# Attention in a four-layer decoder trunk: transposes of probabilities and their products with values, two PSUM banks per step

## The chip, the cores and the metric

The kernel runs on one core of a Trainium2 chip. The metric is the device time of one execution in microseconds. The core has a matrix engine (TensorE; PE in the profile, with PEld for its weight loads), VectorE (DVE), ScalarE (ACT), GpSimd (POOL), and SyncE (SP), whose queue issues most DMAs. Each engine works through its own list of instructions in order. Matrix products and transposes run on PE and write to PSUM, which has 8 banks of 128 partitions by 512 fp32 values.

## The reference

Four layers over an input of 512 tokens by 1024 channels. Each layer is an RMS norm, a token mixer and a residual sum, then a norm, a conv-gated feed-forward block and a residual sum. The mixers are dilated attention (8 heads, three groups), latent attention (16 heads), differential attention (8 heads with two softmax maps each), and sliding-window attention (16 query heads, 2 key heads). Every mixer ends in a product of softmax probabilities with values. The differential one, cut to its core:

```python
def diff_attention(h, w_in, q_norm, k_norm, ..., subln, w_out, table, layer_idx):
    proj = h @ w_in
    q = rms_norm(proj[..., :qk_w].reshape(b, s, DIFF_HEADS, 2, HEAD_DIM), q_norm)
    k = rms_norm(proj[..., qk_w:2 * qk_w].reshape(b, s, DIFF_HEADS, 2, HEAD_DIM), k_norm)
    ...
    def block(args):
        ...
        logits = jnp.einsum('bqhmd,bkhmd->bhmqk', q_blk, k) * (HEAD_DIM ** -0.5)
        logits = jnp.where(dist >= 0, logits + bias, -jnp.inf)
        p = jax.nn.softmax(logits, axis=-1)
        a = p[:, :, 0] - lam * p[:, :, 1]
        return jnp.einsum('bhqk,bkhe->bqhe', a, vf)
    ...
    o = rms_norm(o, subln) * (1.0 - lam_init)
    return o.reshape(b, s, DIFF_HEADS * 2 * HEAD_DIM).astype(h.dtype) @ w_out
```

## The kernel before

The layers run as eight stages one after another: m0, f0, m1, f1, m2, f2, m3, f3 (m is a mixer, f a feed-forward block). Big products split each fp32 operand into a high and a low part and add three products, so names come in pairs (`wh`/`wl` for weights, `xh`/`xl` for the input, `oh`/`ol` for a mixer's output, `qh`/`ql` for queries or keys).

Each stage is written as cooperating generators ("tasks"). `round` advances all live tasks by one step, and a step ends at a `yield`. Buffers come from rings: `take` waits until one of the ring is free, `give` frees one. PSUM has four rings: `a` (3 banks, big products), `lg` (2, logits), `tr` (2, transposes), `av` (1, products with values). A row `a<-wh,xh` of the profile is thus a product into a bank of ring `a`. The tasks give the order in which the program is written. After that, a list scheduler of the language with its own estimate of times sets the final order of instructions on each engine, so moving a step can move rows on every engine, the DMA issues on SP among them.

One head of a mixer runs through these steps, here with the lines of m2:

- The input products land in a bank of ring `a`; `head_norm` (L843 to L853: a reduce on DVE, a chain of small rows, and the product with the scale) writes the normalized `nt`.
- `turn` (L863) transposes `nt` into a `tr` bank, once for the query (`mirror`) and once for the key (`ident`), and splits it into `qh` and `ql`. `stack` (L883) copies these by DMA on SP into `sk` tiles. Other DMAs on SP are the bias tiles (`bs`, L441) and the weight tiles (`wraw`, L254).
- `logits`: the products `lg<-sk` (L302, the line of every product); DVE adds the bias and finds the maximum (`p<-lg,bs`, L909); ACT takes the exponential (L284).
- m2 alone: DVE takes the reciprocals of the sums (L1045) and joins the two maps (L1049, L1050).
- `weigh`: it goes over groups of up to four 128x128 blocks of probabilities. It transposes a group into a `tr` bank (L961, `tr<-mirror,p`), ACT copies the bank to an SBUF tile `ptf` (L956; ring of 3), and PE multiplies it with the values into the `av` bank. Each of the three happens one step later than the one before it, for successive groups, so three groups are in hand at a time. Heads of m0, m1, m2 and m3 have 4, 5, 3 and 4 groups; each mixer calls `weigh` 8 times. `turn` numbers keep the heads in order.
- m2 alone: `head_norm` again, over the `av` bank, writes `ot` (L853), and `turn` transposes it (L863, `tr<-ident,ot`) into `oh` and `ol`.

The products with values have 64 columns of the stationary operand in m0, m1 and m3 and 128 in m2. Products of fp32 operands (`av<-ptf,v` and `av<-v,ptf`, `lg<-sk`) appear in the trace as two records where the program has one.

Of the kernel before, what the change touches and what calls it, by code (L numbers as in the profile page):

```python
# [13 lines left out]
AF = mybir.ActivationFunctionType  # L14
# [81 lines left out]
class Builder:  # L96
# [844 lines left out]
    def weigh(self, groups, turn):  # L941


        nc = self.nc
        ng = len(groups)
        tb, th = {}, {}
        while self.weighing != turn:
            yield
        for i in range(ng + 2):
            if i >= 2:  # L950
                yield from groups[i - 2][1](th[i - 2])
                self.give("ptf")
            if 1 <= i <= ng:
                n = 128 * len(groups[i - 1][0])
                th[i - 1] = yield from self.take("ptf")
                nc.scalar.activation(th[i - 1][:, :n], tb[i - 1][:, :n], AF.Copy)  # L956
                self.give("tr")
            if i < ng:
                tb[i] = yield from self.take("tr")
                for j, blk in enumerate(groups[i][0]):  # L960
                    nc.tensor.transpose(tb[i][:, j * 128:(j + 1) * 128], blk, self.mirror)  # L961
            if i == ng + 1:
                self.weighing += 1
            yield
# [962 lines left out]
```

## Time and profile before

| | |
|---|---|
| median of 3 runs | 2389.44 us (2388.29 to 2394.17) |
| profiled execution | 2390.37 us, span 2388.6 us |
| PE busy | 2331.5 us (98%), 16116 records |
| DVE busy | 1769.0 us (74%) |
| ACT busy | 1280.5 us (54%) |
| POOL busy | 315.4 us (13%) |
| mean granted TensorE clock | 0.99 |

All stretches and starts are microseconds from the start of the span. The stages lie at: m0 0 to 341, f0 to 722, m1 to 926, f1 to 1270, m2 to 1546, f2 to 1890, m3 to 2058, f3 to the end; neighbours overlap a little. A granted clock of 1.00 is the full clock of TensorE.

### The profile page before, as it was taken

What the parts mean: (1) busy time and instruction counts of PE and PEld (TensorE: products, weight loads), DVE (VectorE), ACT (ScalarE), POOL (GpSimd) and SP (SyncE); (2) the same over time, 40 slices, a digit from 0 to 9 for tenths busy, and PEclk for the clock granted to TensorE, in tenths of its full rate; (3) what the DMA queues carried; (4) which work ended last, traced back from release to release, by engine and by line L of the source; (5) the groups of instructions that cost most, each with busy time, mean ns of one, the idle gap of its engine ahead of it and who ended that gap; (6) DMA issues with size and microseconds to landing.
All of it is one profiled execution on the core that took longest, in us unless ns stands there. A gap on an engine that the chain in (4) does not pass through costs nothing.

```text
span 2388.6 us, 41006 instructions
## 1 busy us (share of the span) xinstructions
PE 2331.5 (98%) x16116; PEld 2115.6 (89%) x16116; DVE 1769.0 (74%) x3152; ACT 1280.5 (54%) x2378; POOL 315.4 (13%) x242
## 2 busy tenths in 40 slices
PE   8999989999999999999999998899999999999999
PEld 8999969999997768999989997799999987899998
DVE  6565688787768759877786666798777686987775
ACT  5555555444557756544454554464445575644443
POOL 0000022122002102222100000222220000222220
PEclk9999999999999999999999999999999999999999
DMA  5232255554221126555425454455552442655532
GB/s 181 82 98 89 89 141 164 154 150 133 78 93 45 34 65 173 159 154 151 120 94 159 133 137 113 141 162 150 148 149 76 139 108 91 173 159 158 155 115 84
DMA packets 98160, 298.43 MB, mean 125 GB/s; under 512 B 12144, under 2 KB 18480, under 8 KB 97968
## 3 DMA queue, kind: packets, MB, share of 16 engines
q1 hardware_dynamic: 85296, 249.67, 32.9%
q0 software_dynamic: 12672, 46.14, 11.0%
q8 instruction: 127, 2.08, 0.4%
q14 instruction: 65, 0.53, 0.1%
HBM read 273.62 MB, written 4.32 MB: 116 GB/s over the span
## 4 chain that ended last, share of the span: by engine, by line
PE 93%; DVE 3%; ACT 2%; DMA 1%; issue 1%; SPq 0%; POOL 0%; DVEq 0%; ACTq 0%; POOLq 0%
PE a L302 49%; PE tr L302 19%; PE lg L302 17%; PE av L302 3%; PE tr L961 2%; PE tr L863 2%; DVE r L628 1%; ACT wh L239 0%; DMA sk<-ql 0%; DVE wl L242 0%; DMA sk<-qh 0%; ACT xh L456 0%; DVE acc L466 0%; DMA x<-in_x_dram 0%; DVE xl L463 0%
## 5 line engine op out<-in xcount | busy, mean ns | idle before, releaser
L239 ACT ACTIVATE wh<-wraw 128x1024 fp32r<-128x1024 f32 (+3 forms) x357 | 358.0, 1008 | 493.6 <-PE a L302 216.5
L242 DVE TENSOR_TENSOR wl<-wraw,wh 128x1024 fp32r<-128x1024 f32 (+3 forms) x357 | 441.6, 1239 | 150.9 <-ACT wh L239 149.9
L302 PE MATMUL a<-wh,xh 128*128 128x256 f32 (+1 forms) x1088 | 315.0, 290 | 6.3 <-ACT xh L456 6.3
L302 PE MATMUL a<-wl,xh 128*128 128x256 f32 (+1 forms) x1088 | 311.7, 287 | 0.0
L302 PE MATMUL a<-wh,xl 128*128 128x256 f32 (+1 forms) x1088 | 311.0, 287 | 0.3 <-DVE xl L463 0.3
L302 PE MATMUL a<-ch,wh 128*128 128x256 f32 x960 | 271.7, 283 | 0.0
L302 PE MATMUL a<-cl,wh 128*128 128x256 f32 x960 | 271.5, 283 | 0.0
L302 PE MATMUL a<-ch,wl 128*128 128x256 f32 x960 | 271.4, 283 | 0.0
L302 PE MATMUL tr<-hl,wh 128*128 128x512 f32 x656 | 256.1, 390 | 0.0
L302 PE MATMUL tr<-hh,wh 128*128 128x512 f32 x656 | 255.7, 392 | 0.0
L302 PE MATMUL tr<-hh,wl 128*128 128x512 f32 x656 | 250.5, 390 | 0.0
L256 POOL DMA_DIRECT2D fraw<-in_wup_dram x80 | 69.4, 872 | 1196.0 <-DMA fraw<-in_wup_dram 602.2
L302 PEld LDWEIGHTS a<-wh,xh 128*128 128x128 f32 x1088 | 209.5, 193 | 9.1 <-ACT xh L456 6.3
L302 PEld LDWEIGHTS a<-wl,xh 128*128 128x128 f32 x1088 | 209.6, 193 | 1.5 <-issue 0.4
L302 PEld LDWEIGHTS a<-wh,xl 128*128 128x128 f32 x1088 | 208.7, 192 | 2.2 <-issue 0.9
L302 PE MATMUL a<-xh,wh 128*128 128x256 f32 (+1 forms) x704 | 206.5, 293 | 3.3 <-ACT wh L239 3.3
L302 PE MATMUL a<-xh,wl 128*128 128x256 f32 (+1 forms) x704 | 205.9, 293 | 0.0
L302 PE MATMUL a<-xl,wh 128*128 128x256 f32 (+1 forms) x704 | 204.9, 293 | 0.0
L302 PEld LDWEIGHTS a<-cl,wh 128*128 128x128 f32 x960 | 183.8, 191 | 1.4
L302 PEld LDWEIGHTS a<-ch,wh 128*128 128x128 f32 x960 | 183.7, 191 | 1.4
L302 PEld LDWEIGHTS a<-ch,wl 128*128 128x128 f32 x960 | 183.8, 191 | 0.0
L302 PEld LDWEIGHTS tr<-hh,wl 128*128 128x128 f32 x656 | 123.3, 188 | 25.1
(274 smaller groups left out, 5884.9 us busy)
## 6 DMA issues: line engine op xcount, KB each, us to landing
wraw<-in_wup_dram SPq DMA_DIRECT2D x136, 512.0 KB, 3.3
fraw<-in_wup_dram SPq DMA_DIRECT2D x80, 512.0 KB, 3.4
fraw<-in_wup_dram POOLq DMA_DIRECT2D x80, 512.0 KB, 5.9
wraw<-in_w_dram SPq DMA_DIRECT2D x69, 512.0 KB, 3.4
wraw<-in_wd_dram SPq DMA_DIRECT2D x64, 512.0 KB, 3.4
wraw<-in_wd_dram SPq DMA_DIRECT2D x32, 384.0 KB, 3.0
wraw<-in_o_dram SPq DMA_DIRECT2D x24, 384.0 KB, 3.1
sk<-qh SPq DMA_DIRECT2D x68, 128.0 KB, 2.3
```

What stands on the lines that cost most here:

```text
L239: nc.scalar.activation(wh[:, sl], raw[:, sl], AF.Copy)
L242: nc.vector.tensor_tensor(wl[:, sl], raw[:, sl], wh[:, sl].bitcast(F32), op=OP.subtract)
L256: self.nc.gpsimd.dma_start(out=s["tile"][:, :s["n"]], in_=s["plus"], accum_op=OP.add)
L302: self.nc.tensor.matmul(out, a, b, start=start, stop=stop, skip_group_check=True)
L628: nc.vector.scalar_tensor_tensor(t3, half(x, 1), self.cols[:, gain + k:gain + k + 1], half(y, 1), op0=OP.mult, op1=OP.subtract)
L863: self.nc.tensor.transpose(b[:rows, o * 128:(o + 1) * 128], src(c), self.mirror if query else self.ident)
L961: nc.tensor.transpose(tb[i][:, j * 128:(j + 1) * 128], blk, self.mirror)
```

## The change

`weigh` takes its groups two at a time (`twos`; a last one alone where their number is odd). A step now transposes the blocks of two groups into two `tr` banks, or copies two banks into two `ptf` tiles, or multiplies two `ptf` tiles. The loop has ceil(groups/2) + 2 rounds: 4 instead of 6 in m0 and m3, 5 instead of 7 in m1, 4 instead of 5 in m2. The instructions themselves are the same and equally many. Lines behind `weigh` move down by 8 (L961 becomes L969, L1045 becomes L1053).

```diff
--- before.py
+++ after.py
@@ -942,23 +942,31 @@
 
 
         nc = self.nc
-        ng = len(groups)
+        twos = [groups[i:i + 2] for i in range(0, len(groups), 2)]
+        ng = len(twos)
         tb, th = {}, {}
         while self.weighing != turn:
             yield
         for i in range(ng + 2):
             if i >= 2:
-                yield from groups[i - 2][1](th[i - 2])
-                self.give("ptf")
+                for (_, mul), t in zip(twos[i - 2], th.pop(i - 2)):
+                    yield from mul(t)
+                    self.give("ptf")
             if 1 <= i <= ng:
-                n = 128 * len(groups[i - 1][0])
-                th[i - 1] = yield from self.take("ptf")
-                nc.scalar.activation(th[i - 1][:, :n], tb[i - 1][:, :n], AF.Copy)
-                self.give("tr")
+                th[i - 1] = []
+                for (blocks, _), b in zip(twos[i - 1], tb.pop(i - 1)):
+                    n = 128 * len(blocks)
+                    t = yield from self.take("ptf")
+                    th[i - 1].append(t)
+                    nc.scalar.activation(t[:, :n], b[:, :n], AF.Copy)
+                    self.give("tr")
             if i < ng:
-                tb[i] = yield from self.take("tr")
-                for j, blk in enumerate(groups[i][0]):
-                    nc.tensor.transpose(tb[i][:, j * 128:(j + 1) * 128], blk, self.mirror)
+                tb[i] = []
+                for blocks, _ in twos[i]:
+                    b = yield from self.take("tr")
+                    tb[i].append(b)
+                    for j, blk in enumerate(blocks):
+                        nc.tensor.transpose(b[:, j * 128:(j + 1) * 128], blk, self.mirror)
             if i == ng + 1:
                 self.weighing += 1
             yield
```

The scheduler's order changes in many places. Four engines' rows at three places follow, with buffer numbers where rows would read alike. In these rows an x2 counts instructions of the program.

On PE in m2, around the transposes of `ot` of head 5 (`av<-v,ptf` are this head's last products with values, `lg<-sk` the next head's logits, `a<-oh,wh` and the like the layer's output product). Before:

```order
L302 MATMUL a<-ol_13656,wh 128x512
L302 MATMUL a<-oh_13648,wl 128x512
L302 MATMUL a<-oh_13649,wh 128x512
L302 MATMUL a<-ol_13657,wh 128x512
L302 MATMUL a<-oh_13649,wl 128x512
L302 MATMUL lg<-sk 128x256 x2
L302 MATMUL av<-v,ptf 128x128 x3
L863 MATMUL tr<-ident,ot 128x128 x4
L863 MATMUL tr<-mirror,nt 128x128 x4
```

and in the changed kernel (left out are ten more rows of the output product):

```order
L302 MATMUL av<-v,ptf 128x128 x6
L302 MATMUL a<-ol_13653,wh 128x512
L302 MATMUL lg<-sk 128x384 x2
L302 MATMUL lg<-sk 128x128 x2
L302 MATMUL lg<-sk 128x256 x2
L302 MATMUL a<-oh_13645,wl 128x512
L302 MATMUL a<-oh_13646,wh 128x512
...
L302 MATMUL a<-oh_13649,wl 128x512
L302 MATMUL lg<-sk 128x256 x2
L863 MATMUL tr<-ident,ot 128x128 x4
L863 MATMUL tr<-mirror,nt 128x128 x3
```

The last products of head 5 stood directly ahead of the transposes of `ot`; now 14 rows of the output product and eight logit products stand between.

On DVE at the same place (L843 to L853 with `hst` is the norm, L1045 to L1050 join the maps of head 6, L909 is the logits' bias row). Before, and then changed (L1053 to L1058 are the old L1045 to L1050):

```order
L1045 RECIPROCAL hs<-hs 128x8
L1046 TENSOR_SCALAR hs<-hs,lam 128x4
L1049 TENSOR_SCALAR p<-p,hs 128x512
L843 TENSOR_REDUCE hst<-sq 128x4
L1049 TENSOR_SCALAR p<-p,hs 128x384
...
L1050 SCALAR_TENSOR_TENSOR p<-p,hs 128x256
...
L323 SCALAR_TENSOR_TENSOR hst<-hst 128x8
L324 SCALAR_TENSOR_TENSOR hst<-hst 128x4
L324 SCALAR_TENSOR_TENSOR hst<-hst 128x8
L853 TENSOR_TENSOR ot<-av,hst 128x512
L853 TENSOR_TENSOR nt<-a,hst 128x256 x2
```

```order
L323 SCALAR_TENSOR_TENSOR hst<-hst 128x4
L324 SCALAR_TENSOR_TENSOR hst<-hst 128x4
L853 TENSOR_TENSOR ot<-av,hst 128x512
L909 ISA p,hs<-lg,bs 128x256
L909 ISA hs 128x1
L322 TENSOR_TENSOR hst<-hst 128x8
L323 SCALAR_TENSOR_TENSOR hst<-hst 128x8
L324 SCALAR_TENSOR_TENSOR hst<-hst 128x8
L1053 RECIPROCAL hs<-hs 128x8
L853 TENSOR_TENSOR nt<-a,hst 128x256 x2
L1054 TENSOR_SCALAR hs<-hs,lam 128x4
```

The row that writes `ot` stood behind the rows that join the maps of head 6; now it stands ahead of them, and the rows of `nt` stand behind their first one.

On SP in m2, the transfers of one head's query and key (`sk<-qh`, `sk<-ql`: two of each for the query, four of each for the key). Before, and then changed:

```order
L883 DMA sk<-qh 64x512 x2
L883 DMA sk<-ql 64x512 x2
L441 DMA bs<-bias 128x512
L254 DMA wraw<-in_w_dram 128x1024
L441 DMA bs<-bias 128x512
L883 DMA sk<-qh 64x512 x4
L883 DMA sk<-ql 64x512 x4
```

```order
L254 DMA wraw<-in_w_dram 128x1024
L883 DMA sk<-qh 64x512 x2
L883 DMA sk<-ql 64x512 x2
L883 DMA sk<-qh 64x512 x4
L883 DMA sk<-ql 64x512 x4
L254 DMA wraw<-in_w_dram 128x1024 x2
L441 DMA bs<-bias 128x512 x2
```

Two bias tiles and a weight tile stood between the query's transfers and the key's; now they follow all twelve.

On PE in m3, transposes of probabilities with buffer numbers. Before, and then changed:

```order
L961 MATMUL tr_21257<-mirror_101,p_21162 128x128 x2
L961 MATMUL tr_21257<-mirror_101,p_21165 128x128 x2
L302 MATMUL a_21439<-oh1_20270,wh_21123 128x512
L302 MATMUL a_21791<-oh1_20270,wh_21353 128x512
L863 MATMUL tr_21271<-mirror_101,nt_20815 128x128 x4
...
L961 MATMUL tr_21284<-mirror_101,p_21162 128x128
L961 MATMUL tr_21284<-mirror_101,p_21192 128x128
L961 MATMUL tr_21284<-mirror_101,p_21165 128x128
L961 MATMUL tr_21284<-mirror_101,p_21195 128x128
```

```order
L969 MATMUL tr_21257<-mirror_101,p_21162 128x128
L863 MATMUL tr_21271<-mirror_101,nt_20815 128x128 x4
L969 MATMUL tr_21257<-mirror_101,p_21162 128x128
L969 MATMUL tr_21257<-mirror_101,p_21165 128x128 x2
L969 MATMUL tr_21303<-mirror_101,p_21162 128x128
L969 MATMUL tr_21303<-mirror_101,p_21192 128x128
L969 MATMUL tr_21303<-mirror_101,p_21165 128x128
L969 MATMUL tr_21303<-mirror_101,p_21195 128x128
L302 MATMUL av_21344<-ptf_21318,vh_20285 64x256 x2
```

`tr_21257` and the bank two later share one bank of the ring. Before, six other rows stood between the transposes into it (an output product, a norm's transposes, logits); now the next transposes into that bank (`tr_21303`) follow directly.

## Rows read from the trace of the kernel before

**Rows 1.** The page, busy time of each engine (first line), and the chain of work that ended last, its shares by engine (second line).
```profile
PE 2331.5 (98%) x16116; PEld 2115.6 (89%) x16116; DVE 1769.0 (74%) x3152; ACT 1280.5 (54%) x2378; POOL 315.4 (13%) x242
...
PE 93%; DVE 3%; ACT 2%; DMA 1%; issue 1%; SPq 0%; POOL 0%; DVEq 0%; ACTq 0%; POOLq 0%
```

**Rows 2.** Table by stretch, m1 (722 to 926 us) and m2 (1270 to 1546 us): length, then busy us and instructions of each engine, granted clock of TensorE, DMA share, GB/s.
```profile
722.00:926.00 204.00, 197.45 (x1131) 149.78 (x1131) 148.58 (x433) 134.34 (x324) 34.48 (x70) 0.99 0.23 66
1270.00:1546.00 276.00, 253.80 (x1781) 237.74 (x1780) 186.89 (x491) 143.09 (x350) 11.37 (x6) 0.96 0.50 136
```

**Rows 3.** What PE waited for in the whole span: us in total, times, the longest.
```profile
PE lg L302 <- DVE wl L242: 14.4, 3, 5.8
PE tr L863 <- DVE ot L853: 10.2, 2, 6.9
...
PE lg L302 <- DMA sk<-qh: 4.1, 1, 4.1
...
PE lg L302 <- DMA sk<-ql: 1.9, 2, 1.7
```

**Rows 4.** Timeline of PE, two places of m1: start in us, length, line, operation, written tile<-read tiles, rows x columns of the stationary operand, output, records in one run.
```profile
798.22 1.04 PE L961 MATMUL tr<-mirror,p 128*128 128x128 f32 x8
799.18 1.52 PE L302 MATMUL av<-ptf,v 128*64 128x256 f32 x12
800.63 0.38 PE L302 MATMUL a<-wh,lh 128*128 128x256 f32 x1
800.85 0.28 PE L302 MATMUL a<-wl,lh 128*128 128x256 f32 x1
800.97 0.28 PE L302 MATMUL a<-wh,ll 128*128 128x256 f32 x1
...
832.76 0.65 PE L302 MATMUL av<-ptf,v 128*64 128x256 f32 x4
...
833.93 0.65 PE L302 MATMUL av<-ptf,v 128*64 128x256 f32 x4
```

**Rows 5.** Timeline of PE in m2, around 1363 and 1375 to 1385 us; in brackets the idle time before a row and what ended it.
```profile
1362.99 0.47 PE L302 MATMUL lg<-sk 128*128 128x512 f32 x1 [1.72 <-DMA sk<-ql]
...
1374.33 0.83 PE L302 MATMUL av<-v,ptf 128*128 128x128 f32 x6
1375.00 0.60 PE L863 MATMUL tr<-ident,nt 128*128 128x128 f32 x4
...
1380.83 0.28 PE L302 MATMUL a<-wh,xl 128*128 128x256 f32 x1
1385.24 0.47 PE L302 MATMUL lg<-sk 128*128 128x512 f32 x1 [4.13 <-DMA sk<-qh]
```

**Rows 6.** Timeline of SP's DMA issues in m2 (start and length of the issue, not of the transfer).
```profile
1375.81 0.59 SPq L441 DMA_DIRECT2D bs<-bias  x1
...
1377.54 2.44 SPq L883 DMA_DIRECT2D sk<-qh  x4
```

**Rows 7.** Table by stretch as in rows 2, four stretches of m2.
```profile
1363.00:1366.00 3.00, 3.00 (x23) 2.84 (x24) 0.27 (x1) 0.16 (x1) 0.00 (x0) 1.00 0.79 237
1385.00:1389.30 4.30, 4.06 (x20) 4.05 (x21) 0.00 (x0) 0.00 (x0) 0.00 (x0) 0.60 0.23 65
1457.50:1467.70 10.20, 5.74 (x18) 4.87 (x19) 6.51 (x21) 2.17 (x6) 0.00 (x0) 0.50 0.17 40
1470.00:1500.00 30.00, 30.00 (x157) 25.42 (x156) 21.95 (x50) 15.38 (x32) 0.00 (x0) 1.00 0.49 147
```

**Rows 8.** Timeline of PE in m2, around the transposes of `ot` of head 5.
```profile
1454.24 0.83 PE L302 MATMUL av<-v,ptf 128*128 128x128 f32 x6
1461.96 1.12 PE L863 MATMUL tr<-ident,ot 128*128 128x128 f32 x4 [6.89 <-DVE ot L853]
```

**Rows 9.** Timeline of DVE over the same time.
```profile
1455.54 0.20 DVE L1045 RECIPROCAL hs<-hs 128x8 f32<-128x8 f32 x1 [0.67 <-ACT p L284]
...
1456.44 0.68 DVE L843 TENSOR_REDUCE hst<-sq 128x4 f32<-128x512 f32 x1
...
1460.02 0.48 DVE L1050 SCALAR_TENSOR_TENSOR p<-p,hs 128x256 f32<-128x256 f32 x1
...
1461.21 0.69 DVE L853 TENSOR_TENSOR ot<-av,hst 128x512 f32<-128x512 f32 x1
```

**Rows 10.** Timeline of PE in m2, the transposes of `ot` of the last head.
```profile
1507.51 0.66 PE L863 MATMUL tr<-ident,ot 128*128 128x128 f32 x4 [3.36 <-DVE ot L853]
```

**Rows 11.** Timeline of PE in m2, head 6.
```profile
1469.71 0.60 PE L863 MATMUL tr<-ident,nt 128*128 128x128 f32 x4
...
1474.46 0.40 PE L302 MATMUL lg<-sk 128*128 128x512 f32 x1
...
1476.99 0.39 PE L302 MATMUL a<-oh,wh 128*128 128x512 f32 x1
1477.22 0.39 PE L302 MATMUL a<-ol,wh 128*128 128x512 f32 x1
```

**Rows 12.** Timeline in m3, one row each of DVE, PE and ACT.
```profile
1956.10 0.48 DVE L909 CUSTOM_DVE_ANT_0 p<-lg,bs,nsink 128x256 f32<-128x256 f32 x1
...
1956.17 0.60 PE L961 MATMUL tr<-mirror,p 128*128 128x128 f32 x4
...
1956.81 0.60 ACT L956 ACTIVATE ptf<-tr 128x512 f32<-128x512 f32 x1 [0.34 <-PE tr L961]
```

## The prediction

> **What bounds the kernel now.** I read the page's totals and chain first. TensorE (PE) is busy for 2331.5 of 2388.6 us and is 93% of the chain that ended last [rows 1]. So a change counts only by PE time that it removes or by the 57 us in which PE is idle. Then I read the table by stage: the second layer's attention (m1, 722 to 926 us) has PE busy for 197.45 of 204, and the third layer's (m2, 1270 to 1546 us) for 253.80 of 276, at a granted clock of 0.96 [rows 2]. m2 alone holds 22.2 of the 57 idle us. The list of what PE waited for names three waits there: the transposes of `ot` wait for DVE (two times, 10.2 us), and logit products `lg<-sk` for DMAs (4.1 and 1.9 us) [rows 3]. The biggest wait, `lg<-DVE wl` (14.4), and the others lie where one stage hands over to the next; the change doesn't reach them.
>
> The number of transposes, copies and products stays as it is. The change only moves them, so its price lies in the switches between kinds of work on PE, and in waits.
>
> **Fewer visits to the products (a).** In m1 before, PE alternates between four records of the 64-column products (two products, two passes each) and four transposes: one turn lasts 833.93 - 832.76 = 1.17 us. Where eight transposes and then twelve such records stand in one piece, the eight last 799.18 - 798.22 = 0.96 and the twelve 800.63 - 799.18 = 1.45, so four of each cost 0.96 [rows 4]. A visit thus costs 0.21 more than its work. The row behind the twelve records starts 0.22 later, where its neighbours are 0.12 apart (800.85, 800.97), another 0.10, so a visit between such products may cost 0.31. I take 0.25, nearer the alternation, since that is what pairs remove. In the order, runs of products go from 28 to 22 in m0, 38 to 36 in m1 and 31 to 27 in m3: 12 visits, -3.0 us (bounds -2.5 and -3.7). m2 has 28 to 20, but its products have 128 columns and leaving them shows no gap: the transposes at 1375.00 start 0.67 after six records at 1374.33, 0.11 for each [rows 5]. That costs nothing either way.
>
> **The wait at 1385 us (b).** The k transposes of one head of m2 stand at 1375.00, the last `a` product starts at 1380.83, and the next `lg<-sk` at 1385.24, after 4.13 us of idling on `sk<-qh` [rows 5]. SyncE (SP) shows why: ahead of the eight k transfers (from 1377.54) it issues a bias tile, a weight tile and another bias tile, from 1375.81 on: 1.73 us of issue time, and their data ahead in the queues [rows 6]. In the order of the changed kernel these three stand behind all twelve `sk` transfers, and the k transposes come earlier beside the paired products: between them and that `lg<-sk` stand 81 `a` rows of 0.12 us and logits of 1.06, 10.8 us, instead of 46 rows, 5.5 us. The transfers landed 1385.24 - 1375.00 = 10.2 us after the transposes with the three ahead, 8.5 without them. So the 4.13 us go. What follows ran at a granted clock of 0.60 for 4.3 us [rows 7], which is 1.7 us more. Together -5.8; the low bound is -1.7, the queue's share alone.
>
> **The wait at 1363 us (c)** is 1.72 us [rows 5]. The weight tile that was ahead of its k transfers moves behind their first half, but the cover, counted as in (b), falls from 6.8 to 5.7 us. I take -1.2, between 0 and -1.7.
>
> **Head 5 of m2 (d).** The last products of head 5 start at 1454.24 and directly behind them stand the transposes of its normalized output `ot`, which start at 1461.96 after 6.89 us idle [rows 8]. What DVE does meanwhile decides: the norm's reduce (1456.44) to `ot` (1461.21) is interleaved with the weighting of head 6's probabilities, from 1455.54 to 1460.50 [rows 9]. The last head has no such neighbour, and there the same chain ended after 3.36 us of idle time [rows 10]. In the changed order both sides move: the last six products of head 5 go in one piece, and 14 `a` products of 512 columns (0.23 each, [rows 11]) and logits of 1.1 us stand between them and the transposes, 4.3 us; and on DVE `ot` comes ahead of head 6's reciprocal. The chain of 3.36 us plus some 1.5 for the `p<-lg,bs` rows that stand between (up to 0.48 each [rows 12]) is 4.9, 0.6 more than the cover. Then the `nt` transposes wait, since their `nt` on DVE stands behind the reciprocal, which waits for the last logits' exponential: a bias row, an exponential put at the same 0.48, the reciprocal's 0.20 and two half rows of the size of `ot`'s 0.69 make 1.85 [rows 9, 12], of which 0.6 is counted already, so about 1.2 more. So 6.89 becomes 1.8: -5.1. The granted clock was 0.50, the lower of its two levels (1.2 GHz), from 1457.5 to 1467.7, over which PE was busy for 5.74 us [rows 7]; at full clock that is half, and I give back 2.7. The reason to count it: after the idle times of 1.72 us the clock stayed at 1.00 (1363 to 1366), after 4.13 and 6.89 it fell [rows 5, 7, 8]; 1.8 is near the former. Together -7.8, bounds -2 (the `nt` wait takes most, and the clock falls) and -9.6.
>
> The rule that speaks against this clock term is in the Trainium skill, TensorE: Matmul & The Clock Gate, section "A second HAM failure mode: psum-queue depth-cycling": going round the PSUM banks makes short idle gaps between groups of products, and the clock swings between its two levels. If that were the cause here, pairs would go round banks as before, the 4.4 us of clock in (b) and (d) would not come back, and the sum would be 2381.1 instead of 2376.7. The rows speak for long waits as the cause: 0.99 in m1, where the transposes cycle two banks all the time [rows 2].
>
> **What gets worse (e, f).** (e) Behind head 5, the k transposes start at 1469.71, and the `lg<-sk` that needs their transfers at 1474.46, 4.75 us later and with no idle time [rows 11]: 4.75 was enough. In the changed order 3.2 us of work stand between. What is missing is at most 1.5; I take +1.1, since nothing shows that 4.75 was more than it needed.
> (f) A pair holds both `tr` banks until the ACT copies have freed them. Where the next transposes stand close behind, they wait for a copy. In m3 four transposes at 1956.17 had their copy from 1956.81 to 1957.41: 1.24 us from the first transpose on, of which their own four slots take 0.4, so about 0.9 behind them [rows 12]. The changed order has one place in m3 with no work between (+0.9) and two in m1 with 0.1 and 0.4 us between (0.8 and 0.5, less 0.1 for one with 0.8 that goes: +1.2). In m3 two logit products follow at 0.47 us on those whose bank they take, and the bank is free only after DVE's row of 0.48 and its start [rows 12]: +0.7 each. Their `sk` transfers have 3.7 us of cover where (e) had 4.75, mostly the same wait. Together +3.5, of which 0.5 is taken off for copies that come sooner than this one: +3.0 (0 to 5).
>
> **Sum** against the profiled execution of 2390.37 us (span 2388.6, 1.8 around it; 0.9 above the median of 2389.44): -3.0 - 5.8 - 1.2 - 7.8 + 1.1 + 3.0 = -13.7, so **2376.7 us**. All best bounds give 2369.6, all worst 2390.7.
>
> **The rivals.**
> 1. One of the two long waits of m2 stays: a different transfer or row of DVE comes last. Without (d) and (e): 2383.4; without (b): 2382.5. For it: both rest on orders of several engines. Against: cover grows by 5.3 us in (b).
> 2. The waits move on: PE is earlier in m2, but DVE (busy 186.89 of 276 there [rows 2]) and the transfers don't get faster, and later heads wait instead. Then (b) to (e) give 0 and (a) is eaten by (f): 2390.4. For it: the end of the stage hangs on the last head's chain. Against: from 1470 to 1500 PE is never idle, and DVE was busy for 21.95 of 30 us [rows 7].
> 3. Slower: both banks in one pair's hands make every second step's transposes wait. There are 40 such steps (1 per head in m0, m2 and m3, 2 in m1). At 0.9 us each 36 us are lost and (a) gained: 2423. From 15 steps on (13.7 / 0.9) it eats the forecast's whole gain, from 23 on the kernel is measurably slower. Against: in the changed order only the three places of (f) have under 0.5 us of PE work between.
>
> **How the numbers follow.** Forecast, 2370 to 2383: 0.64. Rival 1: 0.13. Rival 2: 0.15. Rival 3: 0.08. A measurement tells a change from none at about 0.3%, 7.2 us, which is 2382.3. The forecast is faster almost whole; rival 1 lies at the border and goes half to each; rival 2 is the same. Faster 0.69, same 0.23, slower 0.08. The range from 2369 to 2389 leaves out rival 3, the worse half of rival 2 and a little below.
>
> **What would show it.** In the changed trace, the `lg<-sk` after 81 `a` rows starts without idling, and no clock drop follows; `ot` transposes of head 5 wait for under 2 us, and the granted clock there is 1.00; the stage m2 is about 13 us shorter, m1 and m0 within 2 us of before, m3 up to 2 longer, with a wait of transposes for the ACT copy. I am wrong if m2's PE idle time stays near 22 us, or if `tr<-mirror,p` waits for copies appear in many heads.

## The result, and the profile after

The changed kernel takes 2377.54 us (median of 5 runs, 2376.96 to 2379.91) against 2389.44 (2387.89 to 2394.17) on the same chip: a ratio of 0.9946, 95% interval 0.9935 to 0.9957. The profiled execution took 2377.44 us, its span 2375.5. The forecast was 2376.7.

The page, with the lines that answer to [rows 1], busy time and the chain by engine:

```profile
PE 2328.8 (98%) x16116; PEld 2116.3 (89%) x16116; DVE 1773.8 (75%) x3152; ACT 1279.8 (54%) x2378; POOL 310.6 (13%) x242
...
PE 95%; DVE 3%; ACT 1%; issue 1%; DMA 0%; SPq 0%; DVEq 0%; ACTq 0%
```

PE's busy time is 2.7 us shorter and the span 13.1: most of the gain is idle time. The stages m1 and m2 in the table of [rows 2]:

```profile
722.00:926.00 204.00, 196.94 (x1127) 149.82 (x1126) 148.86 (x432) 133.29 (x321) 34.08 (x70) 0.99 0.23 67
1270.00:1546.00 276.00, 265.78 (x1885) 248.65 (x1884) 197.62 (x505) 152.29 (x362) 11.55 (x8) 0.98 0.51 144
```

In the same 276 us around m2 PE is busy for 12 us more, since what comes behind has moved into the stretch, and the granted clock went from 0.96 to 0.98. m1 stands where it stood. What PE waited for, as in [rows 3]:

```profile
PE tr L863 <- DVE ot L853: 3.6, 2, 3.4
...
PE tr L969 <- ACT ptf L961: 1.5, 3, 0.8
PE lg L302 <- DVE hs L909: 1.4, 2, 1.1
...
PE lg L302 <- DMA sk<-ql: 0.4, 1, 0.4
```

The waits of m2 for `ot` fell from 10.2 to 3.6, and those for the `sk` transfers from 6.0 to 0.4 (and 0.4 more that stand under "issue", below at 1458.25). Two lines are new, transposes that wait for the ACT copy (1.5) and logits that wait for DVE's row on their bank (1.4).

Since the program's output products and feed-forward products are the same in both traces, the start of each can be compared with its twin's. The differences, as medians over such rows of PE in a stretch, give the gain stage by stage:

| stretch | PE's rows start earlier (-) or later (+) by its end | share of the stretch |
|---|---|---|
| m0, before its last wait | -0.7 | -0.7 |
| m0's last wait and what follows | +0.9 | +1.6 |
| hand-over to f0, f0 | -0.2 | -1.1 |
| m1 | +0.1 | +0.3 |
| hand-over to f1, f1 | +1.1 | +1.0 |
| m2 up to 1395 | -5.8 | -6.9 |
| m2 up to head 5 | -6.2 | -0.3 |
| m2, head 5 and behind | -14.4 | -8.3 |
| hand-over to f2, f2 | -14.3 | +0.1 |
| m3 | -12.3 | +2.0 |
| hand-over to f3, f3 | -12.6 | -0.3 |

The spans differ by 0.5 more, outside these rows.

The two places in m2 on PE and SP, first the one that answers to [rows 5, 6]:

```profile
1379.22 0.63 PE L302 MATMUL lg<-sk 128*128 128x512 f32 x2
```

```profile
1372.05 2.47 SPq L883 DMA_DIRECT2D sk<-qh  x4
...
1377.19 1.02 SPq L254 DMA_DIRECT2D wraw<-in_w_dram  x2
1378.26 0.92 SPq L441 DMA_DIRECT2D bs<-bias  x2
```

No idle time stands ahead of the `lg<-sk`, and the weight and bias tiles follow the transfers. Then head 5, as in [rows 8, 9, 11], on PE and on DVE:

```profile
1442.08 1.50 PE L302 MATMUL av<-v,ptf 128*128 128x128 f32 x12
...
1448.10 0.63 PE L863 MATMUL tr<-ident,ot 128*128 128x128 f32 x4 [0.27 <-DVE ot L853]
...
1449.52 0.33 PE L863 MATMUL tr<-mirror,nt 128*128 128x128 f32 x1 [0.57 <-DVE nt L853]
...
1453.93 0.60 PE L863 MATMUL tr<-ident,nt 128*128 128x128 f32 x4
...
1458.25 0.47 PE L302 MATMUL lg<-sk 128*128 128x512 f32 x1 [0.42 <-issue]
```

```profile
1444.24 0.69 DVE L843 TENSOR_REDUCE hst<-sq 128x4 f32<-128x512 f32 x1 [2.78 <-ACT sq L840]
...
1447.27 0.69 DVE L853 TENSOR_TENSOR ot<-av,hst 128x512 f32<-128x512 f32 x1
...
1448.97 0.20 DVE L1053 RECIPROCAL hs<-hs 128x8 f32<-128x8 f32 x1 [0.19 <-ACT p L284]
1449.09 0.70 DVE L853 TENSOR_TENSOR nt<-a,hst 128x256 f32<-128x256 f32 x2
```

The `ot` transposes waited 0.27 us instead of 6.89, the `nt` transposes behind them 0.57. On DVE `ot` is written ahead of the reciprocal. The stretch around it ran at the full clock:

```profile
1446.00:1456.00 10.00, 9.16 (x49) 7.32 (x48) 8.87 (x29) 4.82 (x16) 0.00 (x0) 1.00 0.42 106
```

And the waits that are new, one of m1 and two of m3, on PE:

```profile
756.55 0.66 PE L969 MATMUL tr<-mirror,p 128*128 128x128 f32 x4 [0.44 <-ACT ptf L961]
...
1939.79 1.32 PE L302 MATMUL lg<-sk 128*128 128x128 f32 x8 [1.14 <-DVE hs L909]
...
1942.84 0.66 PE L969 MATMUL tr<-mirror,p 128*128 128x128 f32 x4 [0.85 <-ACT ptf L961]
```

### The profile page after: what moved, and what is told of

The parts are those of the page before. It is cut to its first block, busy times and chain, and to the rows that moved or that the text cites. A ratio compares the mean times of both kernels' runs of the same rounds, so it can differ in the third digit from the quotient of the medians.

```text
span 2375.5 us, 41007 instructions
## 1 busy us (share of the span) xinstructions
PE 2328.8 (98%) x16116; PEld 2116.3 (89%) x16116; DVE 1773.8 (75%) x3152; ACT 1279.8 (54%) x2378; POOL 310.6 (13%) x242
## 3 DMA queue, kind: packets, MB, share of 16 engines
HBM read 273.62 MB, written 4.32 MB: 117 GB/s over the span
## 4 chain that ended last, share of the span: by engine, by line
PE 95%; DVE 3%; ACT 1%; issue 1%; DMA 0%; SPq 0%; DVEq 0%; ACTq 0%
PE a L302 51%; PE tr L302 19%; PE lg L302 17%; PE av L302 3%; PE tr L969 2%; PE tr L863 2%; DVE r L628 0%; DVE wl L242 0%; ACT p L284 0%; DVE p L909 0%; ACT wh L239 0%; DVE x L452 0%; DVE acc L466 0%; DMA x<-in_x_dram 0%; PE lg L1288 0%
## 5 line engine op out<-in xcount | busy, mean ns | idle before, releaser
L242 DVE TENSOR_TENSOR wl<-wraw,wh 128x1024 fp32r<-128x1024 f32 (+3 forms) x357 | 446.6, 1253 | 139.9 <-ACT wh L239 138.7
L302 PE MATMUL a<-wh,xh 128*128 128x256 f32 (+1 forms) x1088 | 313.7, 289 | 6.3 <-ACT xh L456 6.3
L302 PE MATMUL a<-wl,xh 128*128 128x256 f32 (+1 forms) x1088 | 311.4, 286 | 0.0
L302 PE MATMUL a<-wh,xl 128*128 128x256 f32 (+1 forms) x1088 | 310.4, 286 | 0.0
L302 PE MATMUL a<-ch,wh 128*128 128x256 f32 x960 | 271.6, 283 | 0.0
L302 PE MATMUL a<-cl,wh 128*128 128x256 f32 x960 | 271.5, 283 | 0.0
L302 PE MATMUL a<-ch,wl 128*128 128x256 f32 x960 | 271.4, 283 | 0.0
L302 PE MATMUL tr<-hl,wh 128*128 128x512 f32 x656 | 256.2, 390 | 0.0
L302 PE MATMUL tr<-hh,wh 128*128 128x512 f32 x656 | 255.6, 392 | 0.0
L302 PE MATMUL tr<-hh,wl 128*128 128x512 f32 x656 | 250.4, 390 | 0.0
L302 PEld LDWEIGHTS a<-wh,xh 128*128 128x128 f32 x1088 | 208.7, 192 | 9.4 <-ACT xh L456 6.3
L302 PEld LDWEIGHTS a<-wl,xh 128*128 128x128 f32 x1088 | 208.9, 192 | 2.1 <-issue 0.9
L302 PEld LDWEIGHTS a<-wh,xl 128*128 128x128 f32 x1088 | 208.0, 192 | 2.3 <-issue 1.1
L302 PE MATMUL a<-xh,wh 128*128 128x256 f32 (+1 forms) x704 | 206.6, 293 | 2.3 <-ACT wh L239 2.3
L302 PE MATMUL a<-xh,wl 128*128 128x256 f32 (+1 forms) x704 | 206.0, 293 | 0.0
L302 PE MATMUL a<-xl,wh 128*128 128x256 f32 (+1 forms) x704 | 205.1, 293 | 0.0
L302 PEld LDWEIGHTS a<-cl,wh 128*128 128x128 f32 x960 | 183.9, 192 | 1.4
L302 PEld LDWEIGHTS a<-ch,wh 128*128 128x128 f32 x960 | 183.8, 191 | 1.4
L302 PEld LDWEIGHTS a<-ch,wl 128*128 128x128 f32 x960 | 183.9, 192 | 0.0
L302 PEld LDWEIGHTS tr<-hh,wl 128*128 128x128 f32 x656 | 123.3, 188 | 25.1
```

The source lines that it names most:

```text
L242: nc.vector.tensor_tensor(wl[:, sl], raw[:, sl], wh[:, sl].bitcast(F32), op=OP.subtract)
L302: self.nc.tensor.matmul(out, a, b, start=start, stop=stop, skip_group_check=True)
```

## The experiments

Some of these kernels have a few more lines, so that a row's line number is 3 or 4 higher in them (L305 is the old L302, L866 the old L863, L973 the old L969). "Shift" is that of PE's rows against the kernel before, as in the table above.

**Which stage holds the gain.** The change with a number of groups per step for each mixer:

```diff
+PAIRS = (1, 1, 2, 1)
...
     def mixer2(self):
+        self.per_step = PAIRS[2]
...
-        twos = [groups[i:i + 2] for i in range(0, len(groups), 2)]
+        k = self.per_step
+        twos = [groups[i:i + k] for i in range(0, len(groups), k)]
```

Pairs in m2 alone:

> Pairs in the differential mixer (m2) alone; the other three mixers take one group per step as before. Theory: m2 holds the whole gain. In the changed kernel's trace the start of f2 against the start of m2 is 15.4 us earlier than before, m3 is 2.0 us longer and m0 with its hand-over about 0.2 shorter, m1 with its hand-over 1.3 longer. So m2 alone should give 2389.4 - 15.4 = 2374.0 us, some 3 faster than the changed kernel. Rival (fewer visits to 64-column products give 3 us that the new waits don't eat): m2 alone is slower than the changed kernel, about 2379 to 2380.

Measured: 2374.22 us, ratio to the kernel before 0.9933 (0.9921 to 0.9946). The trace's shift over m2 and its hand-over is -16.7 us (-15.3 in the second trace of the same program, further down), and m3 is as it was before, with none of the changed kernel's waits for copies. PE's waits in m3:

```profile
PE lg L305 <- DVE wl L245: 4.2, 1, 4.2
PE lg L305 <- issue: 0.4, 1, 0.4
PE tr L973 <- DVE ql L298: 0.2, 1, 0.2
PE a L305 <- ACT oh L296: 0.2, 1, 0.2
```

Pairs in m0, m1 and m3, `PAIRS = (2, 2, 1, 2)`:

> Pairs in m0, m1 and m3, one group per step in m2. Theory: what fewer visits give (-3.0) goes into the new waits for ACT copies and banks (+3.0) and a clock drop that now follows m0's last wait (1.7): 2389 to 2392 us, no gain; the two long waits of m2 (4.1 and 6.9 us) stand as before. Rival (fewer visits count by themselves): 2386.4.

Measured: 2390.83 us, ratio 0.9999 (0.9990 to 1.0008). Over the whole span PE waited for:

```profile
PE tr L866 <- DVE ot L856: 10.2, 2, 6.9
...
PE lg L305 <- DMA sk<-qh: 4.3, 2, 3.7
...
PE tr L973 <- ACT ptf L965: 1.5, 3, 0.8
```

Both long waits of m2 are back, 6.9 and 3.7 us where [rows 3] had 6.9 and 4.1. The shift is -0.7 over m0, again, and +2.0 over m3, again. Fewer visits to the products are worth 0.7 in m0, and with the waits nothing in sum.

**The wait at 1385 us, SP's order alone.** The kernel before, with a dependence that only fixes an order on SP's queue:

```diff
+                ins = self.bias_tile(bs, m * 8 + h, B_FULL)
+                if h == 4:
+                    self.behind(ins, [(lastk[4], None)])
...
+            if getattr(self, "hold", None) is not None:
+                self.behind(ins, [(self.hold, None)])
+                self.hold = None
```

The first part holds head 4's bias tiles behind the last `sk` transfer of its key, the second (in the loader of the weight tiles) the first weight tile that is written after it.

> The kernel before (no pairs) with one order fixed on SP: in m2 two bias tiles and the weight tiles go behind the twelve sk transfers of head 4. PE's order is the same up to the logits that waited, so their cover stays at 5.5 us. Prediction's step: the queue's share is 1.73 us, the idle time falls from 4.13 to about 2.4 and the time to 2386 to 2388. Rival (the tiles' data held the key's transfers as well): idle time about 0, no clock drop behind it, 2383 to 2385. Second rival (the time is the transfers' own): 4.1 us stay.

Measured: 2383.54 us, ratio 0.9972 (0.9960 to 0.9983). PE and SP at the place:

```profile
1375.69 0.60 PE L866 MATMUL tr<-ident,nt 128*128 128x128 f32 x4
...
1381.64 0.39 PE L305 MATMUL lg<-sk 128*128 128x512 f32 x1
...
1382.45 0.47 PE L305 MATMUL lg<-sk 128*128 128x512 f32 x1 [0.42 <-DMA sk<-qh]
```

```profile
1378.17 2.39 SPq L886 DMA_DIRECT2D sk<-qh  x4
1380.65 2.48 SPq L886 DMA_DIRECT2D sk<-ql  x4
1383.18 1.08 SPq L254 DMA_DIRECT2D wraw<-in_w_dram  x2
1384.30 1.73 SPq L444 DMA_DIRECT2D bs<-bias  x2
```

PE's order up to that `lg<-sk` is the one of before, and the idle time is gone but for 0.42 us at the next one: the logits start 5.95 us after the key's transposes instead of 10.2. The rival was right, and the prediction's step was not. The key's issues start 2.48 us after the transposes here (1378.17 less 1375.69) and 2.54 before [rows 5, 6], so the three issues ahead did not delay the issue of the transfers that PE waited for. It is their data that delayed. DMA issues between 1374 and 1386 us, size and median time from issue to landing, first of the kernel before and then of this one:

```profile
sk<-qh SPq DMA_DIRECT2D x5, 128.0 KB, 6.8
bs<-bias SPq DMA_DIRECT2D x2, 256.0 KB, 6.1
wraw<-in_w_dram SPq DMA_DIRECT2D x1, 512.0 KB, 6.3
```

```profile
sk<-qh SPq DMA_DIRECT2D x6, 128.0 KB, 2.3
```

1 MB of tiles was in front, and a 128 KB transfer of `sk<-qh`, on which PE waited, took 6.8 us to land instead of 2.3. The Trainium skill, DMA: Bandwidth & Descriptors, section "Queues, rings and completion order", says that the descriptors of a queue are consumed in ring order on each of the DMA engines that they share; the two traces agree.

**Head 5, DVE's order alone.** The kernel before, with head 6's reciprocal behind head 5's `ot` on DVE:

```diff
-            nc.vector.reciprocal(hs[:, 16:24], hs[:, 8:16])
+            ins = nc.vector.reciprocal(hs[:, 16:24], hs[:, 8:16])
+            if h == 6:
+                self.behind(ins, [(written[5], None)])
```

> The kernel before (no pairs) with one order fixed on DVE: head 6's reciprocal in m2 goes behind head 5's row that writes ot. PE's order is the same up to that place, so nothing covers the chain. Theory: the idle time ahead of head 5's ot transposes falls from 6.89 to about 3.4 us, what the last head's chain takes, the clock drop gets shorter: 2384 to 2386 us. Rival (PE work between products and ot transposes is what counts, DVE's order only follows): idle time stays above 6 us and the time at 2389.

Measured: 2386.60 us, ratio 0.9986 (0.9977 to 0.9995), 0.6 above what was expected. PE and DVE at the place, and the clock behind it:

```profile
1452.98 0.83 PE L302 MATMUL av<-v,ptf 128*128 128x128 f32 x6
...
1457.67 1.12 PE L863 MATMUL tr<-ident,ot 128*128 128x128 f32 x4 [3.85 <-DVE ot L853]
```

```profile
1456.92 0.69 DVE L853 TENSOR_TENSOR ot<-av,hst 128x512 f32<-128x512 f32 x1
1457.53 0.19 DVE L1046 RECIPROCAL hs<-hs 128x8 f32<-128x8 f32 x1
```

```profile
1458.00:1463.00 5.00, 4.99 (x16) 3.65 (x15) 5.00 (x13) 1.28 (x2) 0.00 (x0) 0.50 0.05 11
```

3.85 us of idle time are left of 6.89. PE's rows behind head 5 come 2.7 us earlier than ahead of it; the granted clock still fell to 0.50, so nothing came back there. Of the changed kernel's 8.3 us at this place DVE's order thus gives some 3. The other 5 go to what the changed kernel has beside it, work on PE ahead of the `ot` transposes, and with it a clock that stays up. They are a difference: no run has that cover with DVE's old order.

The same trace says how steady the DMA waits of [rows 5] are, since the order on PE and SP is the one of before up to here. At the place of the 4.13 us:

```profile
1381.85 0.77 PE L302 MATMUL lg<-sk 128*128 128x512 f32 x1 [3.12 <-DMA sk<-qh]
```

It is 3.12 us here and 3.69 with pairs in m0, m1 and m3. The wait at 1363, 1.72 us in the trace of before, is 0.57 to 0.85 in the four traces that have the old order of m2 up to there (these two, SP's order alone and both orders). The trace that the prediction was read from had the longest of both.

**Both orders, without pairs.** The two edits above together.

> The kernel before (no pairs) with both orders fixed: SP's tiles behind head 4's transfers, and head 6's reciprocal behind head 5's ot on DVE. Theory (two waits of m2, independent of each other): 2389.4 less 5.8 for the first (as the trace of the first order alone shows between 1290 and 1395 us) and some 4 for the second: 2378.5 to 2381, more than half of the change's gain without a single pair. What is left to m2 with pairs alone (2374.2) is the cover that pairs put ahead of ot, some 5 us. Rival (the second wait comes back once the first is gone, since PE is 6 us earlier at head 5 and DVE isn't): 2383 to 2384.

Measured: 2381.09 us (2379.41 to 2383.41), ratio 0.9967 (0.9955 to 0.9979), 0.1 above what was expected. In its trace PE's rows come 5.8 us earlier behind the first place, as with the first order alone, and 3.2 more behind the second. In both traces some 0.9 of the 5.8 came at the wait at 1363, which neither edit touches. PE's waits between 1290 and 1520 us:

```profile
PE tr L866 <- DVE ot L856: 3.6, 2, 3.4
PE tr L866 <- DVE hst L326: 3.5, 1, 3.5
```

3.5 us at head 5 remain (the row under `hst`, a row of the same chain), the chain without cover. By the ratios 0.33% of the time goes without a single pair, about 60% of the 0.54% that the change gave; by the shift over m2 and its hand-over it is 9.9 us of 15.4. The intervals are wide, and the share is rough.

**Another shake of the same order.** The kernel before with one constant:

```diff
-GAPS = (10, 12, 10, 12)
+GAPS = (10, 12, 8, 12)
```

> The kernel before (no pairs) with one constant changed: in m2 the launcher starts heads 8 rounds apart instead of 10. In its order 24 output products and eight logit products happen to stand between head 5's last products and the ot transposes, and head 4's key transfers have one bias tile less ahead and 62 rows of cover. Theory (the gain is one of order, and any step that shakes the order of m2 can give it): both long waits are under 1 us and the time is 2374 to 2379. Rival (pairs themselves are needed): 2387 to 2391.

Measured: 2379.76 us (2377.12 to 2380.54), 0.8 above what was expected, ratio 0.9955 (0.9943 to 0.9968), an interval that overlaps the change's. The shift over m2 and its hand-over is -11.7 us, against -15.4 with the change. PE's waits between 1290 and 1520 us, and head 5 on PE:

```profile
PE tr L863 <- DVE ot L853: 3.8, 2, 3.4
PE lg L302 <- DMA sk<-ql: 1.8, 3, 1.2
PE lg L302 <- DMA sk<-qh: 1.0, 1, 1.0
```

```profile
1441.16 0.83 PE L302 MATMUL av<-v,ptf 128*128 128x128 f32 x6
...
1449.42 0.60 PE L863 MATMUL tr<-ident,ot 128*128 128x128 f32 x4
```

The `ot` transposes of head 5 start without a wait, 8.26 us after the last products (the 3.8 are head 4's 0.4 and the last head's 3.4). The first place is not wholly mended: 1.2 us of waiting remain there (expected was under 1), and other heads' transfers are waited for, 2.8 us in all.

**m0 and m2 paired,** `PAIRS = (2, 1, 2, 1)`:

> Pairs in m0 and m2, one group per step in m1 and m3. Theory: m0 with pairs ends 0.7 us earlier (six visits, 0.12 each, by the changed kernel's trace), m2 16.7 earlier, m1 and m3 as before: 2373.5, the same as pairs in m2 alone within what can be measured. Prediction's price of 0.25 for a visit: 2372.7.

Measured: 2374.94 us, ratio 0.9935 (0.9922 to 0.9947), no difference from m2 alone that the timing can tell. The trace has -0.71 us over m0, to the hundredth what the changed kernel has there.

**The change and pairs in m2 alone, side by side.** Both kernels once more on one chip:

> The changed kernel once more, on the same chip as pairs in m2 alone, to compare the two directly: about 2377.5 us, as measured before. Theory: 3 us slower than pairs in m2 alone, of which 2.0 in m3 and about 0.6 to 1 in m1 and its hand-over, less 0.7 in m0. Rival: no difference beyond 1 us.

> Pairs in m2 alone once more, on the same chip as the changed kernel: about 2374.5 us, 2 to 3 us faster than it. Rival: no difference beyond 1 us.

Measured: 2376.01 us (2374.74 to 2379.40) and 2375.18 (2372.38 to 2375.52), ratios 0.9942 (0.9928 to 0.9956) and 0.9931 (0.9918 to 0.9943). The medians differ by 0.8 us, where 2 to 3 were expected, and the intervals overlap, so by timing this is open; pairs in m2 alone are not shown to beat the change. The traces do show the +2.0 us over m3 with pairs there and nothing without.

## Why the prediction was right

The sum was -13.7, and the profiled executions differ by 12.9 us. Its terms, beside the shifts of PE's rows in the trace after:

| term | predicted | in the trace |
|---|---|---|
| m0, visits (a) | -1.5 | -0.7 |
| m1, visits and waits (a, f) | +0.7 | +0.3 |
| m2, the waits at 1385 and 1363 (b, c) | -7.0 | -6.9 |
| m2, head 5 and the next transfers (d, e) | -6.7 | -8.3 |
| m3, visits and waits (a, f) | +1.3 | +2.0 |
| taken off (f) | -0.5 | |
| m0's last wait; hand-overs and m2 between the places | 0 | +1.6; -0.6 in sum |

- (a) was twice too large for m0: 0.12 for a visit instead of 0.25. The alternation of [rows 4] stands in m1, where products and transposes follow each other at every four rows. In m1 and m3 PE's waits grew by 0.5 and 2.4 us and the shifts are +0.3 and +2.0, which leaves about 0.1 for a visit there too. That is an estimate from the two traces. All 12 visits then gave some 1.3 us instead of 3.0; why so little is not shown.
- (b) had nearly the right size for a partly wrong reason. I gave it to the cover of 10.8 us and priced SP's queue at 1.73 us of issue time. The order on SP alone, with the cover of before, took away all but 0.42 of the 4.13 us. Issue time was nothing, the 1 MB of data ahead was nearly all of it. That the cover would have done it too is not shown. With SP's order alone the place itself gave 4.9 to 5.4 us (by the rows directly behind it, or those from 1400 on), forecast 5.8: the 3.7 of idle time, and the clock, which stayed at 1.00.
- (c) went whole: no `lg<-sk` waits there. But the old order has it at 0.57 to 0.85 us in four traces, and the wait at 1385 at 3.12 and 3.69 in two. So between 1 and 2 us of the -6.9 are the trace of before and not the change, and the nearness to -7.0 is luck.
- (d): the idle time fell to 0.84 us, predicted 1.8; the 1.5 us that I added for the bias rows on DVE were too many, perhaps since they fill gaps in which the norm waits for ACT. The clock stayed at 1.00, and the 2.7 came back. DVE's order and PE's cover both count, some 3 us as measured and 5 by difference.
- (e) cost 0.4 instead of 1.1: 4.32 us after its transposes the `lg<-sk` ran, so 4.75 had been more than it needed.
- (f) was right as to places, in m3 and m1. In m3 the logits waited 1.14 us (predicted 1.4 for both) and the transposes 0.85 (0.9). In m1 the transposes waited 0.7 us in two places together, of the 0.8 and 0.5 predicted.
- The rivals: neither did the waits move on in m2 nor did second steps wait in many places. PE waits for ACT copies 1.5 us in the whole span, three times.
- Had going round the banks been the cause of the low clock, as I weighed, 4.4 us would not have come back. At head 5 the granted clock stayed at 1.00 once the long wait was gone, while the banks were cycled as before. That speaks for the wait as the cause.

The mechanism held in m2, where the gain is, but for the reason given for (b). That the sum came within 0.8 us is partly luck: (a) was too large by some 1.7, (d) too small by 0.9, the clock drop behind m0's last wait put 1.6 on by chance, and the hand-overs, which I held to be out of the change's reach, moved by -1.1 and +1.0 and nearly cancel. Why they moved is open.

One step failed that the sum doesn't show. From 1.72 us without and 4.13 with a clock drop I concluded that the length of a wait decides. Behind m0's last wait the clock fell in the trace after and not before, which cost 1.6 us, and the wait is the same. The section after the next one has the rows.

## What to carry to other kernels

Where a scheduler orders the instructions, cost an edit by its order, place by place: here the pairs by themselves were worth about 0.1 us for each visit saved, which new waits ate up, and the 12 us came from where a DMA, a norm and a row of transposes came to stand. Then ask whether fixed orders give the same without the edit; here two of them gave about 60% of it, and a constant gave most of it. Before a transfer that something waits for, count the bytes that are queued ahead of it, not the issues. And read a wait from more than one trace before it goes into a sum: with the same order one wait was 1.72 us in one trace and 0.57 to 0.85 in four others.

## What the runs showed of the hardware

The last wait of m0 is 2.32 us long in every trace. The table by stretch and the row on PE, of the changed kernel's first trace, and then of the same program's second:

```profile
303.00:316.00 13.00, 10.68 (x43) 8.21 (x42) 7.92 (x12) 6.53 (x12) 1.26 (x1) 0.87 0.02 7
```

```profile
306.96 1.30 PE L302 MATMUL a<-oh,wh 128*128 128x512 f32 x3 [2.32 <-ACT oh L293]
```

```profile
303.00:316.00 13.00, 10.68 (x50) 8.39 (x49) 9.61 (x15) 7.65 (x13) 1.27 (x1) 1.00 0.12 38
```

One program, the same 10.68 us of PE's busy time, and the granted clock is 0.87 in one execution and 1.00 in the other. The kernel with SP's order alone, whose m0 is the one of before, had the drop too:

```profile
303.00:316.00 13.00, 10.68 (x43) 7.96 (x43) 7.00 (x11) 6.10 (x10) 1.28 (x1) 0.87 0.10 37
```

It came in 6 of the 11 traces, with pairs in m0 and without, and stands for the 1.6 us in the shifts. What decides it is open. The drops behind the waits of over 3 us in m2 came in every trace that had such a wait.
